# A macaron decoder trunk: gates of a feature pair moved ahead of the first token-major group, and the down stage's products over both feature ranges in the same banks

## The chip, the cores and the metric

The kernel runs on one core of one Trainium2 chip. The metric is the device time of one execution in microseconds (us). Engines in the text: PE is TensorE's matmul, PEld its weight load, DVE VectorE, ACT ScalarE, POOL GpSimd, SP SyncE, which issues the transfers here. [...]

## The reference

Two layers, each of a feed-forward part, a token mixing part (three attentions, gated) and a second feed-forward part, on 512 tokens of width 1024. The change touches the feed-forward parts alone, four in all:

```python
D_FF = ((8 * D_MODEL // 3 + 127) // 128) * 128          # 2816 = 22 feature tiles of 128

def _swiglu(t, w_gate, w_up, w_down):
    return (jax.nn.silu(t @ w_gate) * (t @ w_up)) @ w_down
...
    for l in range(DEPTH):
        f = _swiglu(_rmsnorm(h, ffn1_pre_g[l]), ffn1_w_gate[l], ffn1_w_up[l], ffn1_w_down[l])
        h = h + 0.5 * _rmsnorm(f, ffn1_post_g[l])
        ...                                             # token mixing
        f = _swiglu(_rmsnorm(h, ffn2_pre_g[l]), ffn2_w_gate[l], ffn2_w_up[l], ffn2_w_down[l])
        h = h + 0.5 * _rmsnorm(f, ffn2_post_g[l])
```

All inputs are fp32.

## The kernel before

**Precision.** Each fp32 operand is split into a high and a low part of type fp32r: a cast on ACT (L188, out `wh`, `ah`, `ag`, `hid`) and a difference on DVE (L189, out `wl`, `al`, ...). A product then takes three matmuls (`mm3`, L214 to L216): high by high, and the two mixed ones. The four feed-forward parts carry the names a0, c0, a1, c1; in the profile's names the digit is left out (pta, ptc).

**Stages of one feed-forward part** (`ffn`). The 22 feature tiles are worked in three ways.

- Tiles 16 and 17 come first, as an "early" pair (`halved`, L811 to L814), in two halves of the tokens, while the input's last tiles are still being normed. Banks `pg`, `pu`.
- Tiles 0 to 15 go in four token-major groups of four tiles (`TG`; `group`, `gate_up`; banks `pt`). A group computes gates and ups together as a 2 x 2 block product with seven block products in place of eight. The left blocks are sums and differences of input blocks, made once per part in three steps (`sums`: `whole` L677, `block_sum` L683, `parts_of`; tiles `r`, `ag`). The right blocks are differences of weight blocks, made per group on DVE (`BlockUnit.load`, L337 to L349; tiles `kt`). Products 2, 3, 5 and 6 need such a difference, 4 takes one that is there, 0 and 1 none. Group 0 runs them in the order 0 to 6, the others in `ORDER` = 0, 2, 3, 4, 5, 1, 6. `SUM` says which of three pairs of banks a product adds to: products 0, 3, 5, 6 the first, product 1 the second (or, where it runs late, banks seeded from SBUF), 2 and 4 the third. Partial sums are evicted to tiles `c` (copies L747 on ACT, adds L749 on DVE). `feature_major` transposes the result (L768) into `hr`, eight pairs of feature tiles.
- Tiles 18 and 19, and 20 and 21, are plain pairs: `gates` (2 x 8 x 3 = 48 matmuls into two banks `pg`), then `ups` (48 matmuls), then `hidden` per tile: silu on ACT (L656), product on DVE (L657), split.

The down projection takes tiles 0 to 15 in two feature ranges of eight tiles (`ci` = 0, 1), each again as seven products in `ORDER`, of 24 matmuls each (`product`, banks `pd` of the tag z; weight blocks `bt`, L337 to L349; `first_factor` makes the left blocks, sums `as` L849 to L855, split into `ah`, `al`). After each product both banks are evicted to the output tiles `f`: copies on ACT (L887) or, where `f` holds something already, adds on DVE (L889). Product 1 starts from banks seeded by ACT (L723). The plain pairs stand between the products: gates 18 behind 0 and 2 of the first range, ups 18 behind 5; gates 20 and ups 20 in the second range. Last, tiles 16 to 21 are projected by `down`, which also norms and adds to the stream `h`.

**What sets the order.** A `Queue` holds jobs (weights needed, generator of matmuls); `Q.add` appends one. When a job starts it loads its own weight units and those of the next jobs, four units ahead. A plain unit or a block unit is 512 KB: fetched by SP into `raw` (two buffers), split into `wh`, `wl` (four buffers each). Kept blocks (`kt`, `bt`) are fetched beside it. The order in which the program emits its instructions is a priority: a planner at compile time with its own costs sets the final order on each engine, and may put a ready instruction ahead of one that waits. After that each engine works its list in order.

**Buffers by tag.** `BUFS` gives the number: k 2 (`ag` of products 2 and 3, then `bt`), tri 2 (`ag` of 4 and 5, then `hr` 6 and 7, in the mixing other things), o 8, v 6 (`kt`, and left blocks of the down stage), rs 1 (`qk` in the mixing), f 4 (`c`, then the output). PSUM banks: four of tag mm (`pg`, `pu`, `pt`), four of tag z (`pd`).

Of the kernel before, what the change touches and what calls it, by code (L numbers as in the profile page):

```python
# [17 lines left out]
P = 128  # L18
# [4 lines left out]
def kernel(  # L23
# [78 lines left out]

    BUFS = {"u": 2, "v": 6, "q": 2, "k": 2, "o": 8, "tri": 2, "raw": 2, "rs": 1, "cs": 1, "wh": 4, "wl": 4, "f": 4}

# [534 lines left out]

    HR = ("o", "o", "o", "o", "o", "o", "tri", "tri")  # L640
    ORDER = (0, 2, 3, 4, 5, 1, 6)
    FIRST = (0, 1, 2, 3, 4, 5, 6)

    def ffn(l, src, wg, wu, wd, dst, name, spare, aside=None):
# [8 lines left out]

        def hidden(f, pg, pu):
            s = tmp(f"s{name}_{f}")
            nc.scalar.activation(s[:], pg[:], AF.Silu)  # L656
            nc.vector.tensor_tensor(s[:], pu[:], s[:], ALU.mult)  # L657
            t = blk("q" if f < EARLY + 2 else "o", f"hid{name}_{f}")
            hid[f] = t[:, 0], t[:, 1]
            split(*hid[f], s[:])  # L660
            if f == NF - 1:
                tc.keep_in_program_order(nc.scalar.preload_act_table_set("natural_log_exp_and_others"))
# [202 lines left out]
        def product(ci, n, uns):  # L865
            if n == 0 and ci == 0:
                dst.begin()
            if n < 6:
                first_factor(ci, ORDER[ORDER.index(n) + 1])
            if n in (0, 2):  # L870
                st["b", SUM[n]] = [pbank("z", f"pd{name}_{ci}_{n}_{e}") for e in range(2)]
            pts = st["b", SUM[n]]
            h, l = st["a", ci, n]
            opens, ends = n in (0, 2), n in (1, 4, 6)
            for un in uns:
                for k in range(un.nk):
                    kk = un.k0 + k
                    for e in range(2):
                        c = slice(e * P, (e + 1) * P)
                        mm3(pts[e][:], h[:, kk, c], l[:, kk, c], un.h[:, k], un.l[:, k], opens and kk == 0,  # L880
                            ends and kk == FC // 2 - 1, free=True)
                        yield 3 * S * PE_US
            i, hf = TO[n]
            for e in range(2):
                f = dst.fs[2 * i + e][:, HF[hf]]
                if n == 1 or ci == 0 and n in (0, 2, 3, 6):
                    nc.scalar.copy(f, pts[e][:])  # L887
                else:
                    nc.vector.tensor_tensor(f, f, pts[e][:], ALU.add)  # L889
            if n == 4:  # L890
                st["b", 1] = seeds("z", f"pd{name}_{ci}_1", [dst.fs[e][:, HF[0]] for e in range(2)])

        def products(ci):

            def make(i, k0):
                if k0 == 0:
                    st["bt", i] = stile([P, 2, 2, S], "k", f"bt{name}_{i}", F32)
                return st["bt", i][:, k0 // 2]

            keep, w = Keep(make), wd[l, ci * FC * P:(ci + 1) * FC * P]  # L900
            for n in ORDER:
                uns = [BlockUnit(n, w, FC // 2, k, 2, S, keep, f"d{name}_{ci}_{n}_{k}") for k in range(0, FC // 2, 2)]
                yield uns, (lambda n=n, uns=uns: product(ci, n, uns))

# [16 lines left out]

        def downs(ci):
            Q.add([], lambda: iter(first_factor(ci, 0) or ()))
            return products(ci)

# [36 lines left out]
        Q.add(pairs[1][0], lambda: gates(20, pairs[1][0]))  # L962
        some(4)
        if aside is not None:
# [797 lines left out]
```

## Time and profile before

| what | value |
|---|---|
| median of 3 runs | 2427.16 us (2426.83 to 2427.58) |
| the profiled execution | 2428.36 us, span 2426.6 us, mean granted clock 0.99 |
| PE busy | 2380.1 us, 98% of the span, 11688 matmuls |
| DVE, ACT, POOL busy | 77%, 58%, 3% |
| DMA | 349.73 MB, mean 144 GB/s |
| the four first groups, 216 matmuls each, with group 1's first two products | 60.7, 60.6, 59.8, 59.6 us |
| down stage of c0, both ranges and plain pairs | 123.1 us |

How to read it: busy times of engines overlap, so they do not add up to the span. A busy PE works at the granted clock; a stretch with a granted clock of 0.50 takes twice the time for the same matmuls. A row of a wait names who waited, for whom, the total in us, the times, and the longest. Rows of the trace's timeline begin with the start in us from the span's start and a duration; in brackets stands the idle time before it and what ended it. "x2" in such a row is two instructions merged.

### The profile page before, as it was taken

Reading aid. Unit: us, or ns where it says so; the run is one execution under the profiler, and the core shown is the slowest. Engines: PE = TensorE matmul, PEld = TensorE weight load, DVE = VectorE, ACT = ScalarE, POOL = GpSimd, SP = SyncE. Lnnn points to the kernel's source line nnn. Section 1 sums busy time; section 2 is a strip of 40 time slices with the busy share of each in tenths; the row PEclk is TensorE's granted clock in tenths of the full one; section 3 lists DMA queues with packets and bytes.
Section 4 is the critical chain, followed back from the end, with each engine's and each line's share of the span. In section 5 each row is a group of like instructions: output and inputs, shape, how many; then the busy total and the mean of one; then the engine's idle time right before and its main releaser. Section 6 shows DMA issues by size and latency. Waiting matters only on the chain.

```text
span 2426.6 us, 31086 instructions
## 1 busy us (share of the span) xinstructions
PE 2380.1 (98%) x11688; PEld 2003.4 (83%) x11688; DVE 1872.7 (77%) x2532; ACT 1402.5 (58%) x2291; POOL 74.1 (3%) x130
## 2 busy tenths in 40 slices
PE   8999999999999999999989999999999999899998
PEld 6788888888888887888878888888888888788887
DVE  8788877678777687788787888676787866788885
ACT  5656555577665554565645664556675655556654
POOL 1000000001010000000000000000001100000000
PEclk9999999999999999999999999999999999999999
DMA  5465475222223454644635555642232244455544
GB/s 174 156 209 156 156 241 159 72 80 75 82 68 121 148 165 131 216 149 154 220 129 183 179 159 175 232 131 79 62 88 79 77 132 140 138 177 179 165 165 165
DMA packets 232603, 349.73 MB, mean 144 GB/s; under 512 B 10730, under 2 KB 117506, under 8 KB 231940
## 3 DMA queue, kind: packets, MB, share of 16 engines
q1 hardware_dynamic: 232352, 347.71, 45.2%
q8 instruction: 92, 1.51, 0.3%
q14 instruction: 59, 0.48, 0.1%
q0 software_dynamic: 96, 0.03, 0.0%
q10 hardware_dynamic: 4, 0.00, 0.0%
HBM read 333.02 MB, written 14.68 MB: 143 GB/s over the span
## 4 chain that ended last, share of the span: by engine, by line
PE 81%; DVE 8%; DMA 4%; ACT 3%; issue 2%; POOL 0%; DVEq 0%; ACTq 0%; POOLq 0%
PE pg L216 3%; PE pg L214 3%; PE pg L215 3%; PE ptc L215 3%; PE ptc L216 3%; PE pta L215 3%; PE ptc L214 3%; PE pta L216 3%; PE pta L214 3%; PE pdc L214 2%; PE pdc L215 2%; PE pdc L216 2%; PE pda L215 2%; PE pda L214 2%; PE pda L216 2%
## 5 line engine op out<-in xcount | busy, mean ns | idle before, releaser
L214 PE MATMUL pg<-us_a,wh_wg 128*128 128x512 f32 x384 | 151.0, 393 | 0.0
L216 PE MATMUL pg<-us_a,wl_wg 128*128 128x512 f32 x384 | 149.7, 390 | 0.0
L215 PE MATMUL pg<-us_a,wh_wg 128*128 128x512 f32 x384 | 149.6, 390 | 0.0
L188 ACT CAST wh_ta<-kta 128x1024 fp32r<-128x1024 f32 x80 | 83.3, 1053 | 92.2 <-DVE kta L337 26.2
L188 ACT CAST wh_tc<-ktc 128x1024 fp32r<-128x1024 f32 x80 | 83.2, 1051 | 88.1 <-DVE ktc L337 24.4
L189 DVE TENSOR_TENSOR wl_tc<-ktc,wh_tc 128x1024 fp32r<-128x1024 f32 x80 | 96.8, 1222 | 35.9 <-ACT wh_tc L188 35.5
L189 DVE TENSOR_TENSOR wl_ta<-kta,wh_ta 128x1024 fp32r<-128x1024 f32 x80 | 96.9, 1222 | 33.6 <-ACT wh_ta L188 33.3
L214 PE MATMUL pta<-wh_ta,aga 128*128 128x512 f32 x256 | 102.9, 404 | 13.6 <-ACT wh_ta L188 11.7
L214 PE MATMUL ptc<-wh_tc,agc 128*128 128x512 f32 x256 | 102.4, 401 | 9.8 <-ACT wh_tc L188 9.8
L215 PE MATMUL ptc<-wl_tc,agc 128*128 128x512 f32 x256 | 102.2, 399 | 3.5 <-DVE wl_tc L189 3.5
L215 PE MATMUL pta<-wl_ta,aga 128*128 128x512 f32 x256 | 102.6, 401 | 3.0 <-DVE wl_ta L189 3.0
L216 PE MATMUL pta<-wh_ta,aga 128*128 128x512 f32 x256 | 101.9, 398 | 0.0
L216 PE MATMUL ptc<-wh_tc,agc 128*128 128x512 f32 x256 | 101.6, 397 | 0.0
L214 PE MATMUL pda<-wh_da,aha 128*128 128x512 f32 x224 | 87.3, 390 | 0.0
L214 PE MATMUL pdc<-wh_dc,ahc 128*128 128x512 f32 x224 | 87.3, 390 | 0.0
L215 PE MATMUL pda<-wl_da,aha 128*128 128x512 f32 x224 | 87.2, 389 | 0.0
L215 PE MATMUL pdc<-wl_dc,ahc 128*128 128x512 f32 x224 | 87.1, 389 | 0.0
L216 PE MATMUL pdc<-wh_dc,alc 128*128 128x512 f32 x224 | 86.8, 389 | 0.0
L216 PE MATMUL pda<-wh_da,ala 128*128 128x512 f32 x224 | 86.8, 389 | 0.0
L216 PEld LDWEIGHTS pg<-us_a,wl_wg 128*128 128x128 f32 x384 | 72.1, 188 | 15.3
L215 PEld LDWEIGHTS pg<-us_a,wh_wg 128*128 128x128 f32 x384 | 72.2, 188 | 14.1
L214 PEld LDWEIGHTS pg<-us_a,wh_wg 128*128 128x128 f32 x384 | 72.1, 188 | 14.1
(543 smaller groups left out, 7522.3 us busy)
## 6 DMA issues: line engine op xcount, KB each, us to landing
raw_ta<-in_ffn_w_gate_dram SPq DMA_DIRECT2D x64, 512.0 KB, 3.8
raw_tc<-in_ffn_w_gate_dram SPq DMA_DIRECT2D x64, 512.0 KB, 3.8
raw_da<-in_ffn_w_down_dram SPq DMA_DIRECT2D x58, 512.0 KB, 3.9
raw_dc<-in_ffn_w_down_dram SPq DMA_DIRECT2D x58, 512.0 KB, 3.5
raw_wg<-in_w_gate_dram SPq DMA_DIRECT2D x48, 512.0 KB, 3.6
kta<-in_ffn_w_up_dram SPq DMA_DIRECT2D x32, 512.0 KB, 5.6
ktc<-in_ffn_w_up_dram SPq DMA_DIRECT2D x32, 512.0 KB, 5.8
raw_wo<-in_w_out_dram SPq DMA_DIRECT2D x24, 512.0 KB, 3.4
```

The source lines that it names most:

```text
L188: both = [nc.scalar.copy(h_ap, src)]
L189: make = lambda: nc.vector.tensor_tensor(l_ap, src, h_ap.bitcast(F32), ALU.subtract)
L214: nc.tensor.matmul(pt, lh, rh, start=start, stop=False, skip_group_check=free)
L215: nc.tensor.matmul(pt, lh, rl, start=False, stop=False, skip_group_check=free)
L216: nc.tensor.matmul(pt, ll, rh, start=False, stop=stop, skip_group_check=free)
```

## The change

The gates of tiles 18 and 19 are computed right behind the early pair, ahead of group 0, and their silu is taken at once (`ahead`), so that the two results wait in SBUF (two of the five buffers of `tmp`) and not in banks. All three steps of the sums are emitted before product 0 of group 0. In the down stage the two ranges alternate product by product (`DOWN` = (0,0), (0,1), (2,0), (2,1), ...; first number the product, second the range); both add to the same banks, which are evicted once, behind the second range. The order there becomes: product 0 of both ranges, the last group's transposes, ups 18, products 2, 3, 4 of both ranges, gates 20, products 5, 1, 6 of both, then ups 20 as before. The kept blocks of range 1 go to tag tri; `hr` 6 and 7 go to rs, which gets a second buffer; the scratch of software DMA is set to 8192 bytes.

```diff
-    BUFS = {..., "rs": 1, "cs": 1, "wh": 4, "wl": 4, "f": 4}
+    BUFS = {..., "rs": 2, "cs": 1, "wh": 4, "wl": 4, "f": 4}
-    HR = ("o", "o", "o", "o", "o", "o", "tri", "tri")
+    HR = ("o", "o", "o", "o", "o", "o", "rs", "rs")
...
-        def hidden(f, pg, pu):
+        def silu(f, pg):
             s = tmp(f"s{name}_{f}")
             nc.scalar.activation(s[:], pg[:], AF.Silu)
+            return s
+
+        def hidden(f, pg, pu):
+            s = silu(f, pg) if pg is not None else st.pop(("silu", f))
...
-        def gates(f, ug):
+        def gates(f, ug, ahead=False):
             st[f] = [pbank("mm", f"pg{name}_{f + m}") for m in range(2)]
             for m in range(2):
                 yield from gemm(st[f][m][:], ug, m, act)
+                if ahead:
+                    st["silu", f + m], st[f][m] = silu(f + m, st[f][m]), None
...
         def product(ci, n, uns):
...
-            if n < 6:
-                first_factor(ci, ORDER[ORDER.index(n) + 1])
-            if n in (0, 2):
-                st["b", SUM[n]] = [pbank("z", f"pd{name}_{ci}_{n}_{e}") for e in range(2)]
+            at = DOWN.index((n, ci)) + 1
+            if at < len(DOWN):
+                first_factor(*reversed(DOWN[at]))
+            if n in (0, 2) and ci == 0:
+                st["b", SUM[n]] = [pbank("z", f"pd{name}_{n}_{e}") for e in range(2)]
...
-            opens, ends = n in (0, 2), n in (1, 4, 6)
+            opens, ends = n in (0, 2) and ci == 0, n in (1, 4, 6) and ci == NC - 1
...
+            if ci < NC - 1:
+                return
             i, hf = TO[n]
             for e in range(2):
                 f = dst.fs[2 * i + e][:, HF[hf]]
-                if n == 1 or ci == 0 and n in (0, 2, 3, 6):
+                if n in (4, 5):
+                    nc.vector.tensor_tensor(f, f, pts[e][:], ALU.add)
+                else:
                     nc.scalar.copy(f, pts[e][:])
-                else:
-                    nc.vector.tensor_tensor(f, f, pts[e][:], ALU.add)
...
+        DOWN = [(n, ci) for n in ORDER for ci in range(NC)]
...
+                        st["bt", ci, i] = stile([P, 2, 2, S], ("k", "tri")[ci], f"bt{name}_{ci}_{i}", F32)
...
         marks["first"] = len(Q.jobs)
+        pairs = [(wpair(wg[l], ND, f * P, f"g{name}_{f}"), wpair(wu[l], ND, f * P, f"u{name}_{f}")) for f in (18, 20)]
+        add_sums()
+        Q.add(pairs[0][0], lambda: gates(18, pairs[0][0], True))
         add_sums()
         todo = turns(TG[0])
-        some(1)
-        add_sums()
-        some(7)
+        some(8)
...
-        pairs = [(wpair(wg[l], ND, f * P, f"g{name}_{f}"), wpair(wu[l], ND, f * P, f"u{name}_{f}")) for f in (18, 20)]
-        todo = downs(0)
+        todo = downs()
         some(2)
-        Q.add(pairs[0][0], lambda: gates(18, pairs[0][0]))
         behind()
-        some(3)
         Q.add(pairs[0][1], lambda: ups(18, pairs[0][1]))
-        some(7)
-        todo = downs(1)
-        some(3)
+        some(6)
+        Q.add(pairs[1][0], lambda: gates(20, pairs[1][0]))
+        some(6)
         norm = aside() if aside is not None else None
-        Q.add(pairs[1][0], lambda: gates(20, pairs[1][0]))
-        some(4)
...
-    nc = _bacc.Bacc("TRN2", target_bir_lowering=False, num_devices=1)
+    nc = _bacc.Bacc("TRN2", target_bir_lowering=False, num_devices=1, dynamic_dma_scratch_size=8192)
```

More of the change, by code (lines that the diff above doesn't have):

```diff
@@ L101, in tmp @@
         return sb.tile([P, S], F32, tag="f32t", bufs=5, name=name)
-    BUFS = {"u": 2, "v": 6, "q": 2, "k": 2, "o": 8, "tri": 2, "raw": 2, "rs": 1, "cs": 1, "wh": 4, "wl": 4, "f": 4}
+    BUFS = {"u": 2, "v": 6, "q": 2, "k": 2, "o": 8, "tri": 2, "raw": 2, "rs": 2, "cs": 1, "wh": 4, "wl": 4, "f": 4}
     def stile(shape, tag, name, dt=F32R):
@@ L867, in product @@
                 dst.begin()
-            if n < 6:
-                first_factor(ci, ORDER[ORDER.index(n) + 1])
-            if n in (0, 2):
-                st["b", SUM[n]] = [pbank("z", f"pd{name}_{ci}_{n}_{e}") for e in range(2)]
+            at = DOWN.index((n, ci)) + 1
[3 more added lines that the diff above has]
+                st["b", SUM[n]] = [pbank("z", f"pd{name}_{n}_{e}") for e in range(2)]
             pts = st["b", SUM[n]]
-            h, l = st["a", ci, n]
-            opens, ends = n in (0, 2), n in (1, 4, 6)
+            h, l = st.pop(("a", ci, n))
+            opens, ends = n in (0, 2) and ci == 0, n in (1, 4, 6) and ci == NC - 1
             for un in uns:
@@ L885, in product, with products, keeper, make @@
                 f = dst.fs[2 * i + e][:, HF[hf]]
-                if n == 1 or ci == 0 and n in (0, 2, 3, 6):
+                if n in (4, 5):
+                    nc.vector.tensor_tensor(f, f, pts[e][:], ALU.add)
+                else:
                     nc.scalar.copy(f, pts[e][:])
-                else:
-                    nc.vector.tensor_tensor(f, f, pts[e][:], ALU.add)
             if n == 4:
[L891 to L903, printed above, removed]
+                st["b", 1] = seeds("z", f"pd{name}_1", [dst.fs[e][:, HF[0]] for e in range(2)])
+        DOWN = [(n, ci) for n in ORDER for ci in range(NC)]
+        def products():
+            def keeper(ci):
+                def make(i, k0):
+                    if k0 == 0:
+                        st["bt", ci, i] = stile([P, 2, 2, S], ("k", "tri")[ci], f"bt{name}_{ci}_{i}", F32)
+                    return st["bt", ci, i][:, k0 // 2]
+                return Keep(make)
+            keeps = [keeper(ci) for ci in range(NC)]
+            for n, ci in DOWN:
+                w = wd[l, ci * FC * P:(ci + 1) * FC * P]
+                uns = [BlockUnit(n, w, FC // 2, k, 2, S, keeps[ci], f"d{name}_{ci}_{n}_{k}") for k in range(0, FC // 2, 2)]
+                yield uns, (lambda n=n, ci=ci, uns=uns: product(ci, n, uns))
         marks, todo = {}, iter(())
@@ L920, in turns, with downs @@
             return iter(jobs)
-        def downs(ci):
-            Q.add([], lambda: iter(first_factor(ci, 0) or ()))
-            return products(ci)
+        def downs():
+            Q.add([], lambda: iter(first_factor(0, 0) or ()))
+            return products()
         ug, uu = (wpair(w[l], ND, EARLY * P, f"{x}{name}_{EARLY}") for x, w in (("g", wg), ("u", wu)))
```

## The prediction

> **What bounds the kernel now.** I read the page first, then TensorE's waits, then stretches of the trace cut at the stages of the feed-forward layers. The first line of the page's busy times, and the waits of PE, longest first:
>
> ```profile
> PE 2380.1 (98%) x11688; PEld 2003.4 (83%) x11688; DVE 1872.7 (77%) x2532; ACT 1402.5 (58%) x2291; POOL 74.1 (3%) x130
> ...
> PE pta L214 <- ACT wh_ta L188: 11.7, 2, 6.7
> PE ptc L214 <- ACT wh_tc L188: 9.8, 2, 4.9
> PE ptc L215 <- DVE wl_tc L189: 3.5, 3, 1.5
> PE pta L215 <- DVE wl_ta L189: 3.0, 2, 1.5
> ```
>
> TensorE is busy 98% of the span, so a change that keeps its 11688 matmuls can only win from its waits. Four waits stand out, one per feed-forward layer (a0, c0, a1, c1), all on pt: the first token-major group. The next view gives a stretch a line: us from and to, length, then busy time (and instructions) of PE, PEld, DVE, ACT, POOL, granted clock, DMA share, GB/s. The first four lines hold 216 matmuls each, from the first product of group 0 to the transposes behind group 1's second product. The fifth is 48 matmuls of the down stage with nothing between them. The sixth is the piece of c0 in which PE stops, the last the whole down stage of c0 with both plain pairs.
>
> ```profile
> 37.92:98.57 60.65, 52.32 (x220) 41.78 (x219) 51.24 (x50) 29.99 (x37) 0.00 (x0) 0.92 0.61 206
> 893.37:954.00 60.63, 53.30 (x219) 42.20 (x217) 49.80 (x48) 29.79 (x37) 0.00 (x0) 0.92 0.50 165
> 1245.82:1305.59 59.77, 53.27 (x218) 42.25 (x217) 49.20 (x48) 28.88 (x36) 0.00 (x0) 0.91 0.52 167
> 2096.15:2155.79 59.64, 52.99 (x218) 42.02 (x217) 49.29 (x48) 29.05 (x36) 0.00 (x0) 0.91 0.51 167
> 1063.53:1074.41 10.88, 10.88 (x49) 9.01 (x48) 8.96 (x9) 7.05 (x10) 0.00 (x0) 1.00 0.78 248
> 893.62:915.47 21.85, 14.61 (x55) 10.87 (x54) 21.85 (x22) 10.85 (x13) 0.00 (x0) 0.84 0.48 167
> 1063.53:1186.61 123.08, 122.06 (x546) 100.64 (x545) 100.31 (x113) 66.39 (x90) 0.00 (x0) 1.00 0.51 160
> ```
>
> The undisturbed matmul takes 10.88/48 = 0.2267 us, so 216 need 48.96. The four stretches exceed that by 11.7, 11.7, 10.8 and 10.7; 0.3 of the first is two small transposes. So 44.6 us are lost in the first groups. The down stage loses 123.08 - 122.06 = 1.0 us. The sixth line says why: DVE works 21.85 of 21.85 us. In detail, c0 on PE and on DVE:
>
> ```profile
> 910.49 1.22 PE L214 MATMUL ptc<-wh_tc,agc 128*128 128x512 f32 x2 [4.90 <-ACT wh_tc L188]
> 913.20 0.80 PE L215 MATMUL ptc<-wl_tc,agc 128*128 128x512 f32 x1 [1.49 <-DVE wl_tc L189]
> ...
> 903.98 2.35 DVE L189 TENSOR_TENSOR wl_tc<-ktc,wh_tc 128x1024 fp32r<-128x1024 f32 x2
> ...
> 907.38 2.35 DVE L340 TENSOR_TENSOR ktc<-ktc,ktc 128x1024 f32<-128x1024 f32 x2
> 909.65 2.35 DVE L189 TENSOR_TENSOR agc<-rc,agc 128x1024 fp32r<-128x1024 f32 x2
> 911.92 2.35 DVE L189 TENSOR_TENSOR wl_tc<-ktc,wh_tc 128x1024 fp32r<-128x1024 f32 x2
> 914.19 1.28 DVE L749 TENSOR_TENSOR cc<-cc,ptc 128x512 f32<-128x512 f32 x2
> ```
>
> PE has finished products 0 and 1 by 910.49 - 4.90 = 905.6. Product 2 has its weights (903.98 + 2.35 = 906.3) but no banks: four banks of the tag mm exist, product 0 keeps two, and product 1's two are free only after L749 at 914.19. So PE takes product 3, whose weights DVE makes last. Starts of DVE rows give its prices: a 128x1024 operation costs (914.19 - 911.92)/2 = 1.14, a 128x512 one about 0.60.
>
> Then the clock. These stretches are 3.41 us long:
>
> ```profile
> 106.16:109.58 3.42, 1.73 (x6) 1.16 (x7) 1.26 (x2) 3.39 (x7) 0.00 (x0) 1.00 0.00 0
> 109.58:112.99 3.41, 3.41 (x9) 2.64 (x9) 1.88 (x6) 3.41 (x7) 0.00 (x0) 0.50 0.55 154
> 283.66:287.07 3.41, 2.69 (x11) 1.59 (x10) 3.41 (x5) 2.28 (x3) 0.00 (x0) 1.00 0.01 2
> 287.07:290.49 3.42, 3.42 (x16) 2.80 (x16) 3.42 (x6) 0.85 (x2) 0.00 (x0) 1.00 0.81 238
> 908.30:911.71 3.41, 1.22 (x2) 0.50 (x2) 3.41 (x4) 3.08 (x4) 0.00 (x0) 0.50 0.00 0
> 911.71:915.12 3.41, 1.93 (x5) 1.54 (x6) 3.41 (x5) 0.00 (x0) 0.00 (x0) 0.50 0.00 0
> 915.12:918.54 3.42, 3.42 (x10) 2.65 (x9) 0.35 (x1) 1.06 (x1) 0.00 (x0) 0.50 0.00 0
> ```
>
> Behind a stretch with PE busy 1.73 of 3.42 the clock is 0.50 for one stretch; behind one with 2.69 it stays 1.00. In c0 it is 0.50 for three, in which PE works 1.22 + 1.93 + 3.42 = 6.57 us at half pace: 3.3 of the 11.7 us are clock, the rest is idle time and its edges.
>
> **The change, part by part.** *Gates of pair 18 ahead of group 0.* 48 matmuls, 48 x 0.2267 = 10.88 us, move from the down stage to where PE starves. With them go two weight fetches on SP's queue, two casts on ACT, two low parts on DVE (2 x 1.14 = 2.28) and the two silus on ACT, now without waiting for the ups. The third part of the sums is emitted before product 0 instead of behind it; its amount is the same. In c0: gates 893.4 to 904.3, product 0 to 909.7, product 1 to 915.2. DVE has product 2's weights at 906.3 + 2.3 = 908.6, 6.6 us early, and the two evictions of product 1 are due when nothing else presses. A wait of two 0.60 operations for product 2's banks remains, or none if product 3 goes first: 0 to 2.5 us, I take 1.5. In a0 PE stood at
>
> ```profile
> 56.08 1.22 PE L214 MATMUL pta<-wh_ta,aga 128*128 128x512 f32 x2 [6.75 <-ACT wh_ta L188]
> 58.78 0.79 PE L215 MATMUL pta<-wl_ta,aga 128*128 128x512 f32 x1 [1.49 <-DVE wl_ta L189]
> ```
>
> for 8.2 us in all, less than the 10.9 that come in; same residue.
>
> The fetches: product 0's raw weights move back one turn of the two-buffer ring, to where product 1's are issued now, 885.33 below. Landing takes 3.8 below, two of them one behind the other at most 7.6, so 893; PE needs them at 904.3. Product 1's casts wait for the gates to give back the ring of four (wh, wl): its second unit from 904.3, cast 1.05, low part 1.14, so 906.5 against a need of 909.7. Then product 2's second fetch: 906.5 + 3.8 + 1.14 + 1.05 + 1.14 = 913.6, needed at 915.2 + 2.7 = 917.9. Hidden, by 4 us; if the landing doubled, 0.
>
> ```profile
> 885.33 1.52 SPq L313 DMA_DIRECT2D raw_tc<-in_ffn_w_gate_dram  x2
> ...
> raw_tc<-in_ffn_w_gate_dram SPq DMA_DIRECT2D x64, 512.0 KB, 3.8
> ...
> L188 ACT CAST wh_ta<-kta 128x1024 fp32r<-128x1024 f32 x80 | 83.3, 1053 | 92.2 <-DVE kta L337 26.2
> ```
>
> *Down stage.* The seven products go pairwise over both feature ranges into the same banks. Evictions fall from 28 to 14: L889's adds from 16 to 4 per layer, 12 x 0.60 = 7.2 us less DVE; L887's copies from 12 to 10 and the seeds from 4 to 2 on ACT. Neither is on PE's path.
>
> ```profile
> L889 DVE TENSOR_TENSOR fc<-fc,pdc 128x512 f32<-128x512 f32 x16 | 10.4, 681 | 0.6 <-PE pdc L216 0.6
> L887 ACT COPY fc<-pdc 128x512 f32<-128x512 f32 x12 | 6.7, 586 | 1.9 <-PE pdc L216 1.9
> ```
>
> The price is order. The cover of gates 18 is gone here, and heavy products stand together. DVE per product, from the code and the two prices: products 2, 3 and 5 have four big and four small operations, 6.9 us; product 4 two and four, 4.7; product 6 four and two, 5.7; 0 and 1 two and two, 3.5. PE needs 24 x 0.2267 = 5.4. The run 2,2,3,3,4,4 therefore asks 2 x (6.9 + 6.9 + 4.7) = 37.0 of DVE, with 1.2 left over from the hidden units before it 38.2, against 32.6 of PE: 5.6 us must be done ahead. Ahead lie products 0,0, the transposes and ups 18, (2 x 5.4 + 1.7 + 10.9) = 23.4 us of PE with 5.8 us of DVE of its own (a first factor 1.2, the ups' low parts 2.3, a hidden unit 1.2, the group's last product 1.1), and the rings allow 11.7 us of products 2 to be made there (weights of the first 4.6, differences of the second 2.3, both first factors 4.8). Followed step by step, the low parts for the second product 3 come ready within 0.1 us of their use. So between 0 and 5.6 us per layer; I take 1.5, nearer to 0, because DVE in this stage keeps the idle time that it has: now 123.08 - 100.31 = 22.8; PE's time falls by 10.9 and DVE's by 7.2 + 2.3 = 9.5. DMA: the two products 2 fetch 4 MB, at the 248 GB/s of share 0.78 above (318 at 1.0) 13 us, and they have the 23.4 us before; hidden, else 2 us. The buffers: hr 6 and 7 move to rs (one more buffer), the second range's kept blocks take tri, which group 12's sums leave before its last two products: no wait. POOL's queue carries the same; the smaller DMA scratch touches only a queue that is nearly empty:
>
> ```profile
> q0 software_dynamic: 96, 0.03, 0.0%
> ```
>
> A second buffer for qk in the mixing can only let POOL go earlier: 0.
>
> Sum against the profiled execution (2428.36, 1.2 above the median 2427.16): -44.6 + 4 x 1.5 + 4 x 1.5 = -32.6, so 2395.8; against the median 2394.6.
>
> [...] The trace's rows say that two short idles, 3.42 - 1.73 = 1.7 us together in one stretch, halve the clock for the next, 1.7 us more. [...]
>
> **Rivals.** *The clock still drops.* If 2.5 us stay idle at product 2 in each layer, 1.7 of clock follow: 4 x 4.2 in place of 4 x 1.5 gives 2405; with the same in the down stage (3.4 + 1.7) 2420. For it: the two evictions and the second units of the ring come at the same moment. Against: DVE is 6.6 us ahead there.
>
> *The down stage becomes DVE's, and it is slower.* If nothing of the heavy run is done ahead, 5.6 us are lost at 2 to 4 and 2 x (6.9 - 5.4) = 3.0 at the pair 5; an idle that long brings three halved stretches, 10.24/2 = 5.1: 13.7 per layer, and 1.5 in group 0. 4 x 15.2 - 44.6 = +16, so 2443. It decides from 44.6/4 = 11.1 us per layer on. For it: 38.2 against 32.6. Against: the 22.8 us of idle DVE and ups 18 just ahead.
>
> *It does not do what it says.* The order on each engine is set by a planner; it may put the gates' matmuls elsewhere, or product 1's late units (they wait for the gates) may shift the hole by a product. An idle of 3.5 us and the three halved stretches (5.1) per layer would stay: -44.6 + 34.4 + 6 = -4, so 2423. Against: PE has nothing else that is ready at that place, and the second units have 913.6 against 917.9.
>
> **How the numbers follow.** Forecast 2394.6 with its own range 2381 (nothing left over: 2427.2 - 44.6 = 2382.6, and 1 of the down stage's present loss) to 2402: 0.67. Clock rival, 2402 to 2420: 0.16. Slower: 0.09. Not as it says: 0.08, of which a quarter within 0.2% (4.9 us, about what a measurement of this kernel tells from no change). So faster 0.67 + 0.16 + 0.05 = 0.88, same 0.03, slower 0.09. The range takes the forecast and the clock rival: 2381 to 2420.
>
> **What would show it.** Right: stretches of 216 matmuls from product 0 of group 0 near 49 to 52 us at clock 1.00 in all four layers; 48 matmuls of pg ahead of them with no wait over 1 us; L889 four times and L887 ten times per layer; PE's waits on wh_ta and wh_tc nearly gone. Wrong: DVE without idle in the run 2,2,3,3 and PE waiting on al or wl there, a clock below 1.00 in the down stage, or pt still waiting for more than 3 us. The halved stretch at 109.58 (ACT's statistics of the memory) should stay: it is not touched.

## The result and the profile after

| kernel | median | range | ratio to before, 95% interval |
|---|---|---|---|
| before (4 runs beside it) | 2427.26 us | 2426.83 to 2427.58 | |
| changed (4 runs) | 2407.18 us | 2404.57 to 2410.51 | 0.9918 [0.9901, 0.9935] |

The changed kernel is faster by 20.1 us, where 32.6 were forecast. The profiled execution took 2410.51 us with a span of 2408.8, the slowest of its four; against the profile of before the span is 17.8 us shorter. Line numbers have moved: the evictions of a group are now L751 and L753, the transposes L772 with their copies L776, the down stage's evictions L896 (adds) and L898 (copies).

First the busy times of the changed kernel, then PE's waits, longest first (who waited, for whom, total us, times, longest):

```profile
PE 2374.4 (99%) x11688; PEld 2002.4 (83%) x11688; DVE 1841.9 (76%) x2484; ACT 1393.4 (58%) x2275; POOL 78.9 (3%) x130
...
PE pda L214 <- ACT wh_da L188: 5.2, 2, 2.7
PE pdc L214 <- ACT wh_dc L188: 4.8, 2, 2.5
PE pta L214 <- ACT wh_ta L188: 4.2, 2, 2.4
PE ptc L214 <- ACT wh_tc L188: 4.0, 2, 3.0
```

The waits of 11.7 and 9.8 us on pt have shrunk to 4.2 and 4.0, and two new ones of the same size stand on pd, in the down stage. The stretches of the first groups (216 matmuls from product 0 of group 0, the columns as in the prediction: us from and to, length, busy time and instructions of PE, PEld, DVE, ACT, POOL, clock, DMA share, GB/s), then two stretches of c0's down stage, the last group's transposes and everything behind them up to the last product:

```profile
48.84:101.60 52.76, 50.25 (x219) 40.45 (x218) 43.38 (x41) 27.07 (x34) 0.00 (x0) 1.00 0.63 210
899.54:954.51 54.97, 51.26 (x217) 41.45 (x216) 41.31 (x39) 25.00 (x31) 0.00 (x0) 0.97 0.54 182
1247.61:1302.36 54.75, 51.35 (x218) 41.41 (x216) 40.65 (x38) 24.94 (x30) 0.00 (x0) 0.97 0.55 183
2094.07:2145.60 51.53, 49.75 (x218) 40.29 (x217) 40.82 (x38) 24.99 (x31) 0.00 (x0) 1.00 0.58 194
...
1074.57:1078.74 4.17, 1.91 (x18) 1.67 (x16) 2.96 (x4) 1.92 (x4) 0.00 (x0) 1.00 0.95 324
1078.74:1204.50 125.76, 125.76 (x555) 103.93 (x556) 100.84 (x122) 73.91 (x112) 0.00 (x0) 1.00 0.56 184
```

Together the first groups took 214.0 us where before they took 240.7 (60.65 + 60.63 + 59.77 + 59.64): 26.7 gained. At 48.96 us for 216 matmuls and 0.3 for the two small transposes of a0, 17.9 are still lost. The sixteen transposes of c0 took 4.17 us for 1.66 of work, which is the new loss; behind them PE is busy 125.76 of 125.76 us. Stage by stage, with every matmul's distance to the next compared with the median of its shape, the down stages lose 14.8 us at and right behind the transposes (idle time and halved clock), against 5.4 at their transposes and gates before. So the ledger of the profiled executions is 27 gained, 9 given back.

**Where c0's first group waits.** SP's queue, with one of its waits in the stretch 876 to 918, then what follows on DVE, ACT and PE (start, duration, in brackets the idle time before and what ended it):

```profile
SPq L313 <- DVE wl_tc L189: 16.1, 4, 10.5
...
887.40 14.73 SPq L313 DMA_DIRECT2D raw_tc<-in_ffn_w_gate_dram  x3
...
902.89 0.37 SPq L313 DMA_DIRECT2D raw_tc<-in_ffn_w_gate_dram  x1
903.35 1.12 SPq L313 DMA_DIRECT2D ktc<-in_ffn_w_up_dram  x2
...
900.51 2.35 DVE L189 TENSOR_TENSOR wl_tc<-raw_tc,wh_tc 128x1024 fp32r<-128x1024 f32 x2
905.54 1.23 DVE L337 TENSOR_TENSOR ktc<-ktc,raw_tc 128x1024 f32<-128x1024 f32 x1 [2.67 <-DMA raw_tc<-in_ffn_w_gate_dram]
911.15 1.23 DVE L340 TENSOR_TENSOR ktc<-ktc,ktc 128x1024 f32<-128x1024 f32 x1 [0.91 <-DMA ktc<-in_ffn_w_up_dram]
912.29 1.22 DVE L189 TENSOR_TENSOR wl_tc<-ktc,wh_tc 128x1024 fp32r<-128x1024 f32 x1
913.43 0.68 DVE L753 TENSOR_TENSOR cc<-cc,ptc 128x512 f32<-128x512 f32 x1
...
912.48 1.04 ACT L188 CAST wh_tc<-ktc 128x1024 fp32r<-128x1024 f32 x1 [1.17 <-DVE ktc L340]
...
913.58 1.37 PE L214 MATMUL ptc<-wh_tc,agc 128*128 128x512 f32 x3 [3.00 <-ACT wh_tc L188]
```

Read it upwards. PE waits 3.00 us for a cast, the cast for product 3's difference (L340), and that for a kept block still on its way: it was issued at 903.35. In SP's list it stands behind the raw fetches of product 2, the last of which left at 902.89, 0.46 us ahead of it, and for these the two raw buffers are held by product 1's weights until DVE has split them at 900.51 to 902.86: the fetch at 902.89 leaves 0.03 us behind that. That split had to wait for the gates, at whose end (899.54) the ring `wh`, `wl` comes back. DVE, full before, now has idle time here (2.67 and 0.91 us), both for transfers. The kept block was also long on its way: 7.8 us from its issue to L340, as one of four fetches that SP issued from 902.22 to 904.47. The median landing of such a block was 5.8 us in the kernel before already:

```profile
ktc<-in_ffn_w_up_dram SPq DMA_DIRECT2D x32, 512.0 KB, 5.8
```

Product 2 is no way out, though its first weights are ready at 909.1, before product 1 ends (913.58 - 3.00 = 910.58): its banks come free only with the evictions L753, which stand on DVE behind L340.

**Where c0's down stage waits.** On PE, ACT and DVE:

```profile
1074.57 1.91 PE L772 MATMUL thc<-ident,cc 128*128 128x128 f32 x16
1078.74 0.50 PE L214 MATMUL pdc<-wh_dc,ahc 128*128 128x512 f32 x1 [2.26 <-ACT wh_dc L188]
...
1073.37 1.05 ACT L188 CAST wh_uc<-raw_uc 128x1024 fp32r<-128x1024 f32 x1 [2.37 <-DMA raw_uc<-in_ffn_w_up_dram]
...
1077.64 1.04 ACT L188 CAST wh_dc<-btc 128x1024 fp32r<-128x1024 f32 x1 [2.25 <-DVE btc L337]
1078.59 2.04 ACT L776 COPY hrc<-thc 128x512 f32<-128x512 f32 x4
...
1074.46 1.23 DVE L189 TENSOR_TENSOR wl_uc<-raw_uc,wh_uc 128x1024 fp32r<-128x1024 f32 x1 [0.40 <-ACT wh_uc L188]
1076.38 1.23 DVE L337 TENSOR_TENSOR btc<-btc,raw_dc 128x1024 f32<-128x1024 f32 x1
```

The planner put one matmul of product 2 ahead of ups 18. It waits for the cast of product 2's weights at 1077.64, this for the difference at 1076.38, which on DVE stands behind the split of the ups' weights at 1074.46, whose cast (1073.37) had waited 2.37 us for its transfer. The four copies out of the transposes' banks stand on ACT behind that same late cast: they start at 1078.59, 2.1 us behind the last transpose (1074.57 + 1.91 = 1076.48).

Here too a fetch leaves when a split gives back its raw buffer. SP, and the split of the ups' first half on DVE:

```profile
1072.29 0.37 SPq L313 DMA_DIRECT2D raw_dc<-in_ffn_w_down_dram  x1
...
1075.71 0.37 SPq L313 DMA_DIRECT2D raw_dc<-in_ffn_w_down_dram  x1
...
1071.03 1.23 DVE L189 TENSOR_TENSOR wl_uc<-raw_uc,wh_uc 128x1024 fp32r<-128x1024 f32 x1 [2.84 <-ACT wh_uc L188]
```

Product 2's two raw fetches go at 1072.29 and 1075.71, which is 0.03 and 0.02 us behind the splits of the ups' two halves (1071.03 + 1.23 = 1072.26, and 1074.46 + 1.23 = 1075.69). The first leaves 4.1 us before the difference that needs it (1076.38 - 1072.29), where the median landing of such a fetch is 3.5 us on this kernel's page, so DVE's list and the held buffer were late together:

```profile
raw_dc<-in_ffn_w_down_dram SPq DMA_DIRECT2D x58, 512.0 KB, 3.5
```

### The profile page after: what moved, and what is told of

Read it like the earlier page. It is cut to its first block, busy times and chain, and to the rows that moved or that the text cites. A ratio compares the mean times of both kernels' runs of the same rounds, so it can differ in the third digit from the quotient of the medians.

```text
span 2408.8 us, 31025 instructions
## 1 busy us (share of the span) xinstructions
PE 2374.4 (99%) x11688; PEld 2002.4 (83%) x11688; DVE 1841.9 (76%) x2484; ACT 1393.4 (58%) x2275; POOL 78.9 (3%) x130
## 4 chain that ended last, share of the span: by engine, by line
PE 83%; DVE 7%; DMA 6%; ACT 3%; issue 2%; SPq 0%; DVEq 0%; ACTq 0%
PE pg L214 3%; PE pg L216 3%; PE pg L215 3%; PE ptc L215 3%; PE ptc L214 3%; PE ptc L216 3%; PE pda L214 3%; PE pda L215 3%; PE pda L216 3%; PE pdc L214 2%; PE pdc L215 2%; PE pdc L216 2%; PE pta L214 2%; PE pta L215 2%; PE pta L216 2%; PE pb L214 2%
```

## The experiments

The kernel before was run beside them: 2428.52 us (12 runs) beside the two halves, the early kept blocks and the held-back product; 2426.2 (7 runs) beside the gates in `o`, the ups ahead of the transposes, both together, and the third raw buffer in the changed kernel; 2426.81 (7 runs) beside the last four. Each ratio is to the runs beside it.

**The two halves apart.** The gates alone: the kernel before with gates 18, their silus and all three sums ahead of product 0; in the down stage gates 18 are taken out, and its order, banks and evictions stay.

```diff
@@ the kernel before @@
...
+        pairs = [... for f in (18, 20)]
         add_sums()
+        Q.add(pairs[0][0], lambda: gates(18, pairs[0][0], True))
+        add_sums()
         todo = turns(TG[0])
-        some(1)
-        add_sums()
-        some(7)
+        some(8)
...
         todo = downs(0)
         some(2)
-        Q.add(pairs[0][0], lambda: gates(18, pairs[0][0]))
```

> Only the gates of pair 18 move ahead of group 0 (with their silu and the sums' third step); the down stage keeps the order of before, without gates 18. In the changed kernel the four first groups still lose about 17.5 us of 44.6, and a new wait of 2.3 to 2.8 us per layer stands behind the last group's transposes. Theory: the new wait belongs to the pairwise order of the down stage, so this kernel has the gain of the first groups alone, -27 us, about 2400, and no wait over 1 us behind the transposes. Rival: the wait comes from the gates that are missing in the down stage, however its products are ordered: about 2409, and the same wait on pd is there.

Measured: 2402.72 us (2402.48 to 2404.94), ratio 0.9898 [0.9883, 0.9913]; near the theory's time, and 4.5 us below the change as a whole, though the intervals of the two ratios overlap. The down stage alone: the changed kernel with gates 18 back behind product 0, and the sums in their old place.

```diff
@@ the changed kernel @@
-        Q.add(pairs[0][0], lambda: gates(18, pairs[0][0], True))
-        add_sums()
         todo = turns(TG[0])
-        some(8)
+        some(1)
+        add_sums()
+        some(7)
...
         todo = downs()
         some(2)
+        Q.add(pairs[0][0], lambda: gates(18, pairs[0][0]))
         behind()
```

> Only the down stage changes: products pairwise over both ranges in the same banks, evicted once; gates 18 stay in the down stage behind product 0 of both ranges. Theory: the 14 evictions that go were off the path and the heavy run 2,2,3,3,4,4 is covered by work done ahead, so nothing moves: 2427, within 3 us, first groups lose 44.6 as before. Rival: the pairwise order itself costs what the changed kernel lost in the down stage (about 9 us): 2436.

Measured: 2435.63 us (2428.74 to 2440.02, 9 runs), ratio 1.0024 [1.0014, 1.0034]. The rival's time: the pairwise down stage costs 7 us by itself (2435.63 against 2428.52) and, less surely, 4.5 behind the gates (2407.18 against 2402.72), and the gates bring some 25. PE's waits with the gates alone, its first group in c0 and two stretches of its down stage (the last transposes, the 72 matmuls behind them), and then with the down stage alone:

```profile
PE ptc L214 <- ACT wh_tc L188: 3.6, 2, 2.3
...
PE pda L216 <- DVE ala L189: 1.9, 2, 1.0
...
897.87:950.62 52.75, 49.74 (x218) 40.26 (x216) 40.19 (x38) 24.23 (x30) 0.00 (x0) 1.00 0.57 189
1071.52:1073.18 1.66, 1.66 (x17) 1.66 (x16) 1.66 (x4) 1.53 (x2) 0.00 (x0) 1.00 0.02 5
1073.18:1091.09 17.91, 16.96 (x76) 13.37 (x75) 17.91 (x22) 15.69 (x25) 0.00 (x0) 1.00 0.36 114
```

```profile
PE ptc L214 <- ACT wh_tc L188: 9.6, 2, 4.9
PE thc L772 <- ACT hrc L776: 4.7, 2, 3.5
```

With the gates alone nothing waits at the transposes (1.66 of 1.66 us); behind them PE is idle 0.95 of 17.91 us, and DVE has not a moment free. With the down stage alone the transposes wait. So the wait at the transposes belongs to the order of the down stage, not to the move of the gates. The move is not free there either: without gates 18 the down stage loses 4 x 2.4 us in the old order, in small waits on `al` and `wl`, where the kernel before lost 5.4. And the first groups' residue (3.8 us in c0 even here) belongs to the gates.

**Four attempts at the waits one by one.** Kept blocks of group 0's products 2 and 3 fetched ahead of the gates' job:

```diff
+        def fetch_kept(self):
+            if self.n in (2, 3) and not self.kept:
+                self.kept = True
+                i = self.n - 2
+                tc.keep_in_program_order(self.block(self.keep.get(i, self.k0), (i, 1)))
...
+        todo = turns(TG[0])
+        todo = list(todo)
+
+        def kept_early():
+            for uns, _ in todo0:
+                for un in uns:
+                    un.fetch_kept()
+        todo0, todo = todo, iter(todo)
+        Q.add([], lambda: iter(kept_early() or ()))
         Q.add(pairs[0][0], lambda: gates(18, pairs[0][0], True))
```

> The changed kernel, with the four kept weight blocks of group 0 (products 2 and 3) fetched on SP's queue ahead of the gates' job, not behind product 2's raw blocks, which wait for the raw buffers. Theory: what is left in the first groups (17.5 us in all) is the late landing of six transfers that are issued within 3 us of each other once product 1's weights are split; with four of them gone ahead the rest lands 4 us after issue, and the first groups lose about 6 us in all: 2396. Rival: the wait is that of product 1's eviction and of the planned order (product 3 ahead of 2), and stays: 2407.

Measured: 2411.02 us (2409.05 to 2414.62), ratio 0.9932 [0.9917, 0.9946]: a miss. The kept blocks are there in time (SP issues no `kt` between 884 and 922) and it does not help, because the raw fetches of product 2 still wait for a buffer. In this kernel's c0, SP:

```profile
889.26 15.19 SPq L313 DMA_DIRECT2D raw_tc<-in_ffn_w_gate_dram  x4
```

The four fetches of this row are spread over 15.19 us, to 904.45; product 2's leave no earlier than in the changed kernel (902.89), or 0.7 us earlier by the start of product 0, which is itself later here (901.40 against 899.54). Next, the gates' split weights in tag `o`, so that the ring `wh`, `wl` is free for product 1 at once:

```diff
         add_sums()
+        for un in pairs[0][0]:
+            un.tags = "o", "o"
         Q.add(pairs[0][0], lambda: gates(18, pairs[0][0], True))
```

> The changed kernel, with the split weights of gates 18 in tiles of the tag o in place of the ring of four wh and wl. Product 1's weights then need not wait for the end of the gates. In the run with the kept blocks fetched early the wait stayed, because product 2's raw blocks were issued only once product 1's weights had been split, behind the gates, and DVE then stood idle for 3.5 us. Theory: that ring is the cause; product 2's raw blocks are issued about 10 us earlier, DVE does not idle, PE waits for at most 1.5 us per first group, and no clock is lost there: first groups lose 4 to 6 us in all, 2396. Rival: the planned order (product 3 ahead of 2, the eviction of product 1 behind product 3's differences on DVE) keeps the wait whatever the transfers do: 2405 to 2411.

Measured: 2399.41 us (2396.27 to 2400.43), ratio 0.9886 [0.9871, 0.9901]; the theory held in kind, with a time 3 us above its 2396. Here the raw buffers came free earlier, because product 1's weights could be split earlier (893.36, where it was 900.51), and product 2's fetches followed: the row of SP that answers to 902.89 above starts at 895.74 (product 0 at 898.19, where it was 899.54). The first groups lose 0.8, 0.65, 0.4 and 0.25 us; the transposes still wait. So the chain from the ring of split weights through the raw buffers to SP holds for the first groups. DVE's split, then SP's fetches, in c0 of this kernel:

```profile
893.36 2.35 DVE L189 TENSOR_TENSOR wl_tc<-raw_tc,wh_tc 128x1024 fp32r<-128x1024 f32 x2
...
895.74 0.37 SPq L313 DMA_DIRECT2D raw_tc<-in_ffn_w_gate_dram  x1
```

For the transposes, two changes of order. The first matmul of product 2 held back behind ups 18:

```diff
-        nc.tensor.matmul(pt, lh, rh, start=start, stop=False, skip_group_check=free)
+        first = nc.tensor.matmul(pt, lh, rh, start=start, stop=False, skip_group_check=free)
+        if pin:
+            tc.keep_in_program_order(first)
...
-                            ends and kk == FC // 2 - 1, free=True)
+                            ends and kk == FC // 2 - 1, free=True, pin=(n, ci, kk) == (2, 0, 0))
```

> The changed kernel, with the first matmuls of product 2 of the first range held behind the ups of 18 in TensorE's list; in the changed kernel the planner puts one of them ahead of the ups. Theory: that one matmul, whose weights come 2.3 to 2.8 us late, is all of the wait behind the transposes; with it go four waits (10 us) and the halved clock behind two of them: about 2395, and no wait of over 1 us between the transposes and product 2. Rival: the ups or product 2 behind them wait as long for their own weights, since DVE and the transfers are late there: 2405 to 2408.

Measured: 2408.27 us (2403.9 to 2414.27), ratio 0.992 [0.9902, 0.9938]. And ups 18 ahead of the transposes:

```diff
         some(2)
-        behind()
         Q.add(pairs[0][1], lambda: ups(18, pairs[0][1]))
+        behind()
```

> The changed kernel, with ups 18 ahead of the last group's transposes. Holding the ups ahead of product 2 moved the wait to the ups: they waited 2.9 to 3.4 us for ACT's copies of the transposes, which stand on ACT behind the cast of product 2's first weights. Theory: that cast, in ACT's fixed order, is late by the chain raw fetch of the ups, its split, product 2's difference; 10.9 us of ups ahead of the transposes cover it. The wait behind the transposes (10.7 us in four layers, and up to 1.7 of clock each) goes: 2395. Rival: the chain is late by more than the ups, or product 2 of the second range then waits for the transposes' result: 2403 or more.

Measured: 2406.61 us (2401.34 to 2406.73), ratio 0.9913 [0.9898, 0.9928]. Neither moved the time. The first came out as its rival had it, the second was a miss: the wait went to another place each time. PE's wait in c0 and c1 in the first and in the second of the two:

```profile
PE puc L214 <- ACT hrc L778: 5.0, 2, 2.9
```

```profile
PE thc L772 <- DVE sc L661: 3.7, 2, 2.8
```

First the ups wait for banks that ACT's copies give back, then the transposes for banks that DVE's hidden product gives back. With weights late, ACT and DVE are late in order, and what PE does next meets a bank that one of them holds, for 5.0 us in c0 and c1 in the first kernel and for 3.7 in the second. Both edits together, the gates in `o` and the ups ahead:

> Both: gates 18's split weights in tag o, and ups 18 ahead of the transposes. Theory: the two gains add, about 10 and 12 us from the changed kernel's 2407: 2385 to 2388. Rival: they share a cause (one late chain of transfers), and the second adds nothing: 2395.

Measured: 2399.11 us (2395.39 to 2401.35), ratio 0.9886 [0.9871, 0.99], the same as with the gates in `o` alone: the second edit adds nothing, as the rival had it, at a time 4 us above the rival's.

**A third raw buffer.** One number in the changed kernel:

```diff
-    BUFS = {..., "raw": 2, "rs": 2, ...}
+    BUFS = {..., "raw": 3, "rs": 2, ...}
```

> The changed kernel with three buffers for raw weights in place of two. Theory: product 2's fetches of group 0 wait for raw buffers that product 1's weights hold; a third buffer frees one of the two, so the first groups lose about 10 us in place of 13 to 17, and the ups' and product 2's weights behind the transposes come somewhat earlier: 2400. Rival: buffers of the fetch are not what is short, and nothing moves: 2405 to 2411.

Measured: 2381.74 us (2377.0 to 2382.75), ratio 0.9809 [0.9793, 0.9826]: 25 us below the changed kernel, far more than either theory had expected. Its first groups, its down stage of c0 behind the transposes, and its fetches in c0:

```profile
48.82:103.23 54.41, 51.64 (x219) 41.66 (x218) 44.00 (x43) 29.78 (x38) 0.00 (x0) 0.97 0.58 194
897.29:946.60 49.31, 49.31 (x218) 40.34 (x217) 42.09 (x40) 26.45 (x32) 0.00 (x0) 1.00 0.54 183
1067.80:1193.02 125.22, 125.22 (x555) 103.64 (x554) 99.10 (x121) 74.59 (x112) 0.00 (x0) 1.00 0.53 178
...
894.81 0.93 SPq L313 DMA_DIRECT2D ktc<-in_ffn_w_up_dram  x2
```

In c0, and in a1 and c1 (whose rows are left out, 49.26 and 49.29), PE is busy without a break: 49.3 us for 216 matmuls, where 48.96 is the bare work. Both losses are gone at once, the first groups' and the transposes'. The two kept blocks leave at 894.81, 2.5 us before product 0 starts, where two left at 903.35, 3.8 us after its start. Only a0 still loses (54.41). With the buffer the planner's order changes as well: no matmul of product 2 stands ahead of the ups any more. That order alone, with two buffers, had moved nothing (2408.27 above). How a held buffer becomes a late use was followed row by row in c0 alone; for the other parts the time and the missing waits speak.

**Is it the change that needs the third buffer?** The same buffer in the kernel before, in the gates alone, and in the down stage alone (the first two also get the DMA scratch of the changed kernel, to make room; what the scratch does by itself was not run, but the other two rows of the table below have it in both columns):

> The kernel before with a third raw buffer (and the DMA scratch of the changed kernel, which makes the room). Theory, the third buffer only pays because the change moved the fetches late against their use: in the kernel before the hole of the first groups is DVE's (busy 21.85 of 21.85 us in c0), so the four stretches of 216 matmuls stay near 60 us and the time stays at 2424 to 2428. Rival, the ring of two was short already and half of the 44.6 us of the first groups came from it: 2405 or less, with stretches under 56 us.

> The gates alone (2402.7) with a third raw buffer. Its trace has 11.3 us of excess in the first groups of c0, a1 and c1 and 4 x 2.4 us at the down stage's pd and pg, where PE waits for DVE's low parts of the second factor and not for a fetch. Theory, the buffer takes the first and not the second: 2391 to 2394, so that the pairwise down stage is worth about 10 us once the transfers are in time (2381.7 with it). Rival, the buffer takes both, and the pairwise order is worth nothing: 2381 to 2385.

> The down stage alone (2435.6) with a third raw buffer. Theory, the pairwise order loses only by late fetches behind the transposes (13 to 15 us of excess and halved clock there): these go, the first groups keep their 11 us each, 2420 to 2425, now faster than the kernel before. Rival, the loss is one of order on ACT and DVE that fetches do not mend: 2432 to 2436.

| | two raw buffers | three raw buffers |
|---|---|---|
| before | 2426.2 to 2428.5 | 2416.08 (2414.73 to 2417.51), 0.9957 [0.9942, 0.9972] |
| down stage alone | 2435.63 | 2415.81 (2414.57 to 2416.8), 0.9955 [0.9941, 0.997] |
| gates alone | 2402.72 | 2382.55 (2378.72 to 2384.41), 0.9814 [0.9797, 0.983] |
| both (the change) | 2407.18 | 2381.74 (2377.0 to 2382.75), 0.9809 [0.9793, 0.9826] |

Reading down the right column: with transfers in time the gates are worth 33.5 us (2416.08 to 2382.55) and the down stage nothing (0.3 and 0.8, inside the spread). In the left one, whose runs stand beside different runs of the kernel before, the gates are worth 24 to 28, and the down stage costs 4 to 9. The buffer itself brings 11 us in the kernel before, 20 in each half and 25 in the change, so 11 of the 25 are not the change's doing. For the kernel before the time lies between the two expectations. The hole of its first groups stays, for it is DVE's; of the 11 us about half come from these groups (in c0, a1 and c1 the granted clock of the group is 0.94, where it was 0.91 and 0.92: two halved windows of 3.41 us where there were three), the rest from small waits all over. Its stretch 892 to 910, in the hole of c0, and the whole first group of c0:

```profile
890.12:948.48 58.36, 52.30 (x220) 41.97 (x219) 49.95 (x49) 28.95 (x34) 0.00 (x0) 0.94 0.46 156
892.00:910.00 18.00, 11.94 (x47) 9.03 (x46) 18.00 (x19) 9.21 (x11) 0.00 (x0) 0.88 0.34 115
```

DVE works 18.00 of 18.00 us there while PE works 11.94, as before with two buffers. For the down stage alone the theory had the direction, and not the buffer's own 11 us. For the gates alone the theory was that the buffer would not touch the down stage's waits on `al`; it did (3.8 us in all became 1.2), and the rival's time came. The stretch that answers to 1073.18 above, 72 matmuls behind c0's transposes:

```profile
1068.79:1085.21 16.42, 16.42 (x75) 13.61 (x74) 16.42 (x21) 13.55 (x22) 0.00 (x0) 1.00 0.35 108
```

DVE is full in it too, but PE waits no longer: what DVE has to do ahead of the stretch is done ahead when the weights are there.

**The best of both.** The changed kernel with the third buffer and the gates' weights in `o`:

> The changed kernel with a third raw buffer and with the split weights of gates 18 outside the ring wh, wl. What the third buffer alone left (2381.7) is a0: 1.48 + 1.85 + 5.00 us, of which 5.00 are a halved clock, with waits for the low part of the weights (4.5 us in 4). Theory, these are waits for the split ring that the gates hold: 2.5 to 3.3 us go, 2378 to 2379.5. Rival, they come from the landing of the first fetches in a0, which start late in this layer whatever the ring: 2381 to 2383.

Measured: 2380.29 us (2379.67 to 2380.97), ratio 0.9809 [0.9795, 0.9824]. The median lies between the expectations and within the spread of the third buffer alone, so this is not told apart by the time. In its profile a0 did as the theory had it: the wait for its weights' low parts fell from 4.5 us to 2.3, and its first group from 54.41 to 51.17; but the 168 matmuls behind the group lost 1.6 us more. These three kernels (2380.29, 2381.74, 2382.55) beat both the kernel before and the changed one, by some 45 and some 25 us, and the runs do not rank them. What remains is a0: those 168 matmuls lose 4 to 7 us in each of the three. Before and after the change they lost 4.2, but elsewhere: there PE waited for ACT's copies of `c` (0.89 and 1.02 us up to 108.82 before, 0.87 and 1.03 up to 111.83 after), and a halved window followed (at 109.58 and at 111.95); with three buffers its longest wait is 2.1 us for a low part of the weights, some 30 us later. Its cause stays open.

## Why the prediction was right and wrong

The sign and the measured time inside the range came out; the forecast of 2394.6 was 12.6 us low. The time lies outside the forecast's own range, which ended at 2402, and inside the one that was widened for the clock rival. The step that failed is the second below: fetches that were priced as hidden.

- **Gates cover the hole: right.** DVE was the limit of the first groups (busy 21.85 of 21.85 us where PE stopped in c0), and 10.9 us of matmuls that need only 2.3 of it filled them. With nothing left over it gave 2427.2 - 44.6 = 2382.6. The gates with a third buffer come to 2382.55, but the agreement is partly chance: the buffer also takes some 5 us of small waits elsewhere, and a0 keeps some 5 (54.41 - 48.96 = 5.45 with the buffer in the change, of which 0.3 are transposes).
- **The fetches, "hidden, by 4 us": this step failed.** The prediction followed product 2's second raw fetch by itself, from the split that frees its buffer to the low part of the weights: ready at 913.6, which is 9.3 us after the start of product 0 (904.3). In the trace it is ready at 912.29 + 1.22 = 913.51, 14.0 us after that start (899.54). The fetch was issued a little late (902.89, so 3.35 after the start, where 906.5 meant 2.2); the rest went on DVE, which stood still for two other transfers, 2.67 us for the first raw unit and 0.91 for the kept block that SP issues last. The prediction had not followed these two. 4.7 us late is more than the 4 of cover. Yet PE's 3.00 us were not spent on this unit: product 2 lacked its banks, and product 3, which could have gone in between, hung on the kept block of 903.35. That block took 7.8 us to its use where the prediction reckoned 3.8 for a landing, so "if the landing doubled, 0" had the right size and looked at one transfer by itself, not at the four fetches that SP issued within 2.3 us. The residue of the first groups was 17.9 us where 4 x 1.5 = 6 had been set.
- **Banks of product 2: half right.** PE did go to product 3 first, as the prediction left open. But product 1's evictions were to come "when nothing else presses", and the first one started at 913.43, 2.85 us after product 1's end, behind the differences that waited for transfers.
- **Down stage: the sum near, the place wrong.** Forecast +6, measured +9.4 in the profiles. It was to fall in the run 2,2,3,3,4,4 by DVE's load; there PE is busy without a break, also where DVE is full. It fell at the transposes in front, by late weights. With three buffers it is 0, so the load of 38.2 against 32.6 us was never the limit, and the DVE-bound rival falls with it.
- **Evictions: right in number, worth nothing.** The changed kernel's page has 8 adds (L896) and 20 copies (L898) for c0 and c1 together, so 4 and 10 per part. DVE's busy time fell by 30.8 us (1872.7 to 1841.9) where 4 x 7.2 = 28.8 were counted from the adds, and it paid nothing: with three buffers the kernel that lacks it is within 0.8 us.
- **Clock: the rival had the size of the miss.** The first rival (2402 to 2420: 2.5 us idle in each layer, then 1.7 of clock, and the same in the down stage) gives the measured time by its prices: 4 x 4.2 = 16.8 us for the first groups, where 17.9 were lost. That is luck in part, for its cause was another: it had the evictions meet the ring's second units on DVE, and the trace has DVE wait for transfers ahead of both; and in the first groups the clock fell in two of the four layers only. Behind idles of 3.00 and 2.42 us in two of the first groups (c0, a1) and of 2.55 and 2.52 at two of the transposes (a0, c1) stand halved stretches of 3.41 us, four in all; behind those of 2.26 and 2.66 at the other transposes (c0, a1) stands none (see the last section). A halved stretch was priced at 1.7 us, half of 3.41; by the distances of the matmuls there it costs 1.6. The fifth, of the memory's statistics, stays at 111.95 as the prediction had it.
- **"Does not do what it says": fell.** The gates run ahead of group 0 without a break; in c0:

```profile
888.66:899.54 10.88, 10.88 (x50) 8.99 (x49) 10.68 (x12) 6.84 (x10) 0.00 (x0) 1.00 0.31 94
```


## What to carry to other kernels

When a stage has too little of something, filling it with other work moves its transfers too, and here the raw fetches left when their staging buffer was given back (0.02 and 0.03 us behind the split), not when they could land in time: follow the issue of each fetch in the queue's list, with what frees the buffer, before calling it hidden. Where one change of order after another only moves a wait of the same size from one place to the next, look for what is late upstream of all of them; here a third staging buffer took away both losses at once. A cost that was measured with one buffer too few (the pairwise down stage, 4.5 to 7 us) is no property of the order: with three it was within 0.8 us of nothing.

## What the runs showed of the hardware

The halved windows of the changed kernel ahead of the last 3.1 us of the span start at 111.95, 231.42, 914.09, 1262.24 and 2269.17, at distances of 119.47, 682.67, 348.15 and 1006.93 us; the granted clock is 0.51 in the 3.41 us from each. In the changed kernel, in pairs of a window of 3.41 us and the one that follows:

```profile
228.01:231.42 3.41, 1.61 (x6) 1.14 (x7) 2.30 (x3) 2.71 (x5) 0.00 (x0) 1.00 1.00 332
231.42:234.84 3.42, 3.42 (x10) 2.65 (x9) 3.42 (x5) 2.38 (x4) 0.00 (x0) 0.51 0.98 366
...
1074.51:1077.92 3.41, 1.96 (x17) 1.67 (x15) 3.00 (x3) 1.16 (x3) 0.00 (x0) 1.00 0.91 307
1077.92:1081.33 3.41, 2.59 (x10) 1.95 (x11) 2.61 (x3) 2.88 (x6) 0.00 (x0) 1.00 1.04 388
1422.66:1426.07 3.41, 1.71 (x16) 1.47 (x14) 2.88 (x3) 0.74 (x3) 0.00 (x0) 1.00 1.01 365
1426.07:1429.48 3.41, 2.46 (x10) 1.81 (x11) 2.48 (x3) 2.88 (x6) 0.00 (x0) 1.00 1.02 368
```

Behind the transposes of a0, with an idle of 2.55 us and PE busy 1.61 of 3.41, a halved window followed; behind those of c0 (2.26 us idle, 1.96 of 3.41 busy) and of a1 (2.66 us, 1.71 of 3.41) none did. The prediction's row had 1.73 busy and then a halved window, so these rows place no limit, and what sets the two cases apart was not shown.

In a halved window matmuls of 128x512 start 0.427 us apart, in c0 six distances in 2.56 us:

```profile
914.75 0.63 PE L215 MATMUL ptc<-wl_tc,agc 128*128 128x512 f32 x1
...
917.31 0.52 PE L215 MATMUL ptc<-wl_tc,agc 128*128 128x512 f32 x1
```

At a clock of 1.00 it is 0.2267, so the same matmuls took 1.88 times as long, not twice. A window of 3.41 us holds 8.0 of them where 15.05 would fit: 1.6 us lost, and 3.1 of the 11.7 us in c0 before, where the prediction had 3.3.

What makes the four runs of the changed kernel spread over 6 us, where the four of the kernel before beside them stay within 0.8, was not shown; the twelve runs of the kernel before beside the first experiments spread over 7.6 us themselves (2425.09 to 2432.72).
